# Attention in a hybrid decoder step: a fifth bank for scores, a per-partition scalar for GpSimd's scaling, and two small steps moved to GpSimd

## The chip, the core and the metric

The kernel runs on one core of a Trainium2 chip. The metric is the device time of one execution in microseconds (us), the median of several executions; lower is better.

## What is computed

One inference step of a two-layer decoder trunk, for a prompt of 2048 positions and eight samples of one position each. Layer 0 has a pooling mixer beside differential attention, layer 1 a gated delta rule beside a spatial-gating MLP. The change is in the attention of the prompt. For each of 6 heads there are two softmaxes, over two halves of the head's 128 channels, and their difference weighs the values:

```python
def diff_core(q, k, v, allowed, lam):
    s = jnp.einsum('bqhcd,bkhcd->bhcqk', q, k).astype(jnp.float32) * (DIFF_DH ** -0.5)
    p = jax.nn.softmax(jnp.where(allowed, s, -jnp.inf), axis=-1)
    attn = p[:, :, 0] - lam * p[:, :, 1]
    return jnp.einsum('bhqk,bkhd->bqhd', attn.astype(v.dtype), v)
```

Here c (0 or 1) is the softmax, and a query position sees the keys up to its own.

## The kernel before

The stages run one after the other: the input projection of layer 0, the attention of the prompt, the output projection of layer 0, then layer 1. The code is written in program order, and a scheduler sets the final order on each engine; every engine works its own queue strictly in that order. TensorE is called PE, VectorE DVE, ScalarE ACT, GpSimd POOL.

`attention` loops over 6 heads and, in each, over 16 query tiles of 128 positions. A tile i needs i+1 blocks of 128 keys, which `attn_tile` takes in 1 to 4 chunks (nch) of up to 512 keys. So of a head's 16 tiles four have one chunk, four have two, four three and four four: 240 chunks in all, and 72 tiles with more than one chunk.

For each chunk and each of the two softmaxes: PE multiplies queries by keys into a bank of PSUM (`sc`, lines 810 and 811, and a mask for the last chunk, 813). DVE takes the negated row maximum of it (`nb`, line 814). ACT writes the exponentials to `p` in SBUF and their sums to `l` (line 815). The chunks of a tile are then weighed against each other by the factors `cf`, an array of 128 partitions by 2 softmaxes by nch chunks, which the code calls f. With more than one chunk DVE takes the minimum m of nb (826), subtracts (827), ACT takes the exponential (828), DVE multiplies the sums by it (830), adds them (831), inverts (832), multiplies the second softmax's inverse by minus lambda (833) and multiplies the factors by the inverses (834).

Then, for each chunk, POOL multiplies the second softmax's half of `p` by its factor (838). For three chunks in four DVE multiplies the first half by its factor and adds the second half in one instruction (841); for the fourth POOL does both (843 and 844). PE transposes the result into a bank `tr` (848), ACT copies it to SBUF (850), and PE multiplies it by the values into a bank `pv` (852), which DVE copies out (853). After every fourth tile `attn_out` transposes four finished tiles into a bank `ot` (785), and ACT scales them (787).

PSUM has eight banks. In the table AT a letter is a bank, but X and Y are two banks each; a kind takes the letters of its string in turn, so scores go through X, X, D and A, where the two X are the two banks in turn.

Of the kernel before, what the change touches and what calls it, by code (L numbers as in the profile page):

```python
# [10 lines left out]
F32 = mybir.dt.float32  # L11
# [4 lines left out]
ALU = mybir.AluOpType  # L16
# [4 lines left out]
P = 128  # L21
# [24 lines left out]
BO, BR, BU = 2, 2, 4  # L46
DORD = (("out", 6), ("step", 5), ("merge16", 3), ("merge", 3), ("front", 1), ("blocks", 1), ("load", 0))
SP = 0
AT = dict(sc="XXDA", tr="Y", pv="B", ot="C")
W1, W2, WA, WB, WC = "P", "D", "P", "PD", "PD"  # L50
DE = "PDPPPPP"
CM = 1
# [11 lines left out]
class Net:  # L64
# [634 lines left out]
    def lam_const(self):  # L699
        nc, I, c = self.nc, self.I, self.const  # L700
        tmp = ExitStack()
        t = self.pool(tmp, "lam", 1)
        lq = t.tile([P, 4, 64], F32, name="lq")
        nc.sync.dma_start(lq, I["lam_qk"].rearrange("a c d -> a (c d)").broadcast_to([P, 256]))
        pr = t.tile([P, 2, 64], F32, name="lpr")
        for i in range(2):
            nc.vector.tensor_tensor(pr[:, i], lq[:, 2 * i], lq[:, 2 * i + 1], ALU.mult)
        e = c.tile([P, 2], F32, name="lexp")
        nc.vector.tensor_reduce(e, pr, AX.X, ALU.add)
        nc.scalar.activation(e, e, AF.Exp)  # L710

        self.nlam = c.tile([P, 1], F32, name="nlam")
        nc.vector.scalar_tensor_tensor(self.nlam, e[:, 1:2], -LAM0, e[:, 0:1], ALU.add, ALU.subtract)
        tmp.close()
        self.sub_w = c.tile([P, 1], F32, name="subw")
        nc.sync.dma_start(self.sub_w, I["subln_w"].rearrange("a d -> d a"), allow_slow_non_contiguous=True)

        nc.vector.tensor_scalar(self.sub_w, self.sub_w, 0.5 * (1.0 - LAM0), None, ALU.mult)
        self.at = c.tile([P, NS, self.NJ, NH], F32, name="at")
        self.an8 = c.tile([NS, NH], F32, name="an8")  # L720
        self.tab = c.tile([1, NS * self.NJ], I32, name="tab")
        nc.sync.dma_start(self.tab, I["page_table"].rearrange("b j -> (b j)")[None, :])
        self.maskb = c.tile([P, P], BF16, name="maskb")
        nc.gpsimd.memset(self.maskb, 0.0)
        nc.gpsimd.affine_select(self.maskb, self.maskb, pattern=[[-1, P]], compare_op=ALU.is_ge, fill=NEG, base=0,
                                channel_multiplier=1)

    def attention(self):
        st = ExitStack()
        nc, I = self.nc, self.I  # L730
        self.banks = AT

# [58 lines left out]
    def attn_tile(self, i, kvt, qt, o, oss, pp, tp, sm):  # L791
        nc = self.nc
        mm = nc.tensor.matmul
        nk = i + 1
        nch = (nk + 3) // 4
        q0 = (i % 4) * P
        nb = sm.tile([P, 2, 4], F32, tag="nb", name="nb")
        l = sm.tile([P, 2, 4], F32, tag="l", name="l")
        pc = []
        with self.tc.high_priority(SP) if SP else nullcontext():  # L800
            for j in range(nch):
                n = min(512, nk * P - 512 * j)
                w = max(n, 256)
                kh, kl = kvt[j][:2]
                p = pp.tile([P, 2, 512], F32, tag="p", name="p")
                for c in range(2):
                    sc = self.bank("sc", 512)
                    qc = qt[:, c, q0:q0 + P]
                    last = j == nch - 1
                    mm(sc[:, :w], qc, kh[:, c, :w], start=True, stop=False)  # L810
                    mm(sc[:, :w], qc, kl[:, c, :w], start=False, stop=not last)  # L811
                    if last:
                        mm(sc[:, n - P:n], self.identb, self.maskb, start=False, stop=True)
                    nc.vector.tensor_reduce(nb[:, c, j:j + 1], sc[:, :n], AX.X, ALU.max, negate=True)  # L814
                    nc.scalar.activation(p[:, c, :n], sc[:, :n], AF.Exp, bias=nb[:, c, j:j + 1],  # L815
                                         accum_out=l[:, c, j:j + 1])
                pc.append((p, n))
        cf = sm.tile([P, 2, 4], F32, tag="cf", name="cf")
        f = cf[:, :, :nch]
        if nch == 1:  # L820
            nc.vector.reciprocal(f, l[:, :, :1])
            nc.vector.tensor_scalar(f[:, 1, :], f[:, 1, :], self.nlam, None, ALU.mult)
        else:
            r = sm.tile([P, 2], F32, tag="r", name="r")
            m = sm.tile([P, 2], F32, tag="m", name="m")
            nc.vector.tensor_reduce(m, nb[:, :, :nch], AX.X, ALU.min)
            nc.vector.tensor_tensor(f, m[:, :, None].broadcast_to([P, 2, nch]), nb[:, :, :nch], ALU.subtract)
            nc.scalar.activation(f, f, AF.Exp)
            lf = l[:, :, :nch]
            nc.vector.tensor_tensor(lf, lf, f, ALU.mult)  # L830
            nc.vector.tensor_reduce(r, lf, AX.X, ALU.add)
            nc.vector.reciprocal(r, r)
            nc.vector.tensor_scalar(r[:, 1:2], r[:, 1:2], self.nlam, None, ALU.mult)
            nc.vector.tensor_tensor(f, f, r[:, :, None].broadcast_to([P, 2, nch]), ALU.mult)  # L834
        pv = self.bank("pv", P)
        for j in range(nch):
            p, n = pc[j]
            nc.gpsimd.tensor_tensor(p[:, 1, :n], p[:, 1, :n], cf[:, 1, j:j + 1].broadcast_to([P, n]), ALU.mult)  # L838
            turn = self.turn()
            if turn % 4 < 3:  # L840
                nc.vector.scalar_tensor_tensor(p[:, 0, :n], p[:, 0, :n], cf[:, 0, j:j + 1], p[:, 1, :n], ALU.mult, ALU.add)  # L841
            else:
                nc.gpsimd.tensor_tensor(p[:, 0, :n], p[:, 0, :n], cf[:, 0, j:j + 1].broadcast_to([P, n]), ALU.mult)
                nc.gpsimd.tensor_tensor(p[:, 0, :n], p[:, 0, :n], p[:, 1, :n], ALU.add)
            pt = self.bank("tr", 4, P)
            nt = n // P
            for t in range(nt):
                nc.tensor.transpose(pt[:, t, :], p[:, 0, t * P:t * P + P], self.ident)
            tt = tp.tile([P, 4, P], F32, tag="pt", name="pt")
            nc.scalar.copy(tt[:, :nt, :], pt[:, :nt, :])  # L850
            for t in range(nt):
                mm(pv, tt[:, t, :], kvt[j][2][:, t, :], start=j == 0 and t == 0, stop=j * 4 + t == nk - 1)  # L852
        nc.vector.tensor_copy(o, pv)
        junk = sm.tile([P, P], F32, tag="junk", name="junk", bufs=2)
        nc.scalar.activation(junk, pv, AF.Square, scale=P ** -0.5, accum_out=oss)  # L855
# [917 lines left out]
```

## Time and profile before

| What | Value |
|---|---|
| median of 3 runs | 3105.16 us (3101.53 to 3109.34) |
| the profiled execution's own time | 3097.32 us |
| its span, first to last instruction | 3095.6 us |
| PE busy over the span | 2800.3 us (90%) |
| DVE busy | 2073.9 us (67%) |
| ACT busy | 1492.5 us (48%) |
| POOL busy | 1663.1 us (54%) |

The span is that of the one execution that the profiler recorded; the time of an execution is 1.7 us longer than its span here. The busy shares are means over stages of different kinds: the attention lies from about 781 to 1390 us of the span. Outside it the change adds two small instructions that make a constant; the scheduler's order also differs in parts of layer 1, whose code is the same. A line of a group or a timeline reads: line, engine, operation, output<-inputs, shape out<-in, count, then times.

### The profile page before, as it was taken

How to read it: one execution, taken by the hardware profiler on the slowest of the kernel's cores; microseconds unless marked ns; L12 is line 12 of the kernel's file. 1: busy time of each engine (PE TensorE's matmuls, PEld its weight loads, DVE VectorE, ACT ScalarE, POOL GpSimd, SP SyncE). 2: the span in 40 equal slices, each digit the busy share in tenths (PEclk: the TensorE clock that was granted, in tenths of full speed). 3: DMA queues.
4: the chain of work that ended last, by engine and by line, in shares of the span. 5: the costliest groups of instructions: out<-in, count | busy, mean ns of one | idle time of the engine just before them, and what ended most of it. 6: DMA issues, size and time to landing. Idle time of an engine off the chain costs nothing. (4 is left out here: it accounts for less than half of the span.)

```text
span 3095.6 us, 57877 instructions
## 1 busy us (share of the span) xinstructions
PE 2800.3 (90%) x20425; PEld 2541.6 (82%) x20425; DVE 2073.9 (67%) x4067; ACT 1492.5 (48%) x4431; POOL 1663.1 (54%) x1223
## 2 busy tenths in 40 slices
PE   8999899999998898989898888999999899858999
PEld 8999798999777777778787878778889888747887
DVE  5465555564898999885677877567787574347662
ACT  6644245534887787762223224455454443334431
POOL 4576546571567866664576654546443244246541
PEclk9999999999999999999999999999999999969999
DMA  4567766655344424217777655435233244468442
GB/s 163 166 197 252 246 217 204 189 183 172 86 106 113 103 62 106 71 54 228 228 248 213 183 179 168 132 105 149 88 88 99 90 94 126 114 168 237 134 126 91
DMA packets 428061, 462.55 MB, mean 149 GB/s; under 512 B 84987, under 2 KB 338340, under 8 KB 427772
## 3 DMA queue, kind: packets, MB, share of 16 engines
q1 hardware_dynamic: 427772, 458.86, 50.0%
q8 instruction: 162, 2.65, 0.4%
q14 instruction: 127, 1.04, 0.1%
HBM read 332.41 MB, written 126.33 MB: 148 GB/s over the span
## 5 line engine op out<-in xcount | busy, mean ns | idle before, releaser
L186 PE MATMUL acc<-bh,whi 128*128 128x346 f32 (+6 forms) x2072 | 689.7, 333 | 42.0 <-DVE cx L1232 32.2
L188 PE MATMUL acc<-bh,wlo 128*128 128x346 f32 (+6 forms) x2072 | 687.3, 332 | 8.8 <-DVE wlo L167 8.2
L187 PE MATMUL acc<-bl,whi 128*128 128x346 f32 (+6 forms) x2072 | 686.3, 331 | 0.0
L186 PEld LDWEIGHTS acc<-bh,whi 128*128 128x128 f32 x2072 | 396.9, 192 | 64.8 <-issue 40.8
L188 PEld LDWEIGHTS acc<-bh,wlo 128*128 128x128 f32 x2072 | 396.4, 191 | 28.3 <-DVE wlo L167 10.2
L187 PEld LDWEIGHTS acc<-bl,whi 128*128 128x128 f32 x2072 | 397.0, 192 | 16.6 <-issue 3.1
L815 ACT ACTIVATE p<-sc,nb 128x512 f32<-128x512 f32 (+3 forms) x480 | 302.0, 642 | 72.8 <-DVE nb L814 62.0
L838 POOL TENSOR_TENSOR p<-p,cf 128x512 f32<-128x512 f32 (+3 forms) x240 | 236.9, 1005 | 184.0 <-DVE cf L834 49.5
L167 POOL TENSOR_TENSOR wlo<-wraw,whi 128x1024 fp32r<-128x1024 f32 (+1 forms) x90 | 218.6, 2432 | 138.7 <-ACT whi L165 138.4
L814 DVE TENSOR_REDUCE nb<-sc 128x1 f32<-128x512 f32 (+3 forms) x480 | 275.8, 597 | 18.5 <-PE sc L811 8.9
L628 POOL TENSOR_TENSOR kp<-kp,at 128x768 f32<-128x768 f32 x120 | 203.0, 1701 | 156.4 <-DMA kp<-in_cache_v 130.2
L550 POOL TENSOR_TENSOR kp<-kp,qb 128x768 f32<-128x768 f32 x88 | 169.7, 1934 | 178.3 <-DMA kp<-in_cache_k 140.2
L186 PE MATMUL acc<-whi,bh 128*128 128x256 f32 x864 | 249.9, 290 | 0.3 <-DVE th L418 0.3
L187 PE MATMUL acc<-wlo,bh 128*128 128x256 f32 x864 | 248.6, 288 | 0.2 <-POOL wlo L167 0.2
L188 PE MATMUL acc<-whi,bl 128*128 128x256 f32 x864 | 248.7, 288 | 0.0
L630 DVE TENSOR_TENSOR sacc<-sacc,kp 128x768 f32<-128x768 f32 x120 | 180.2, 1502 | 83.7 <-POOL kp L628 71.5
L852 PE MATMUL pv<-v,pt 128*128 128x128 f32 x1632 | 220.2, 283 | 15.1 <-ACT pt L850 8.2
L810 PE MATMUL sc<-kh,q 128*128 128x512 f32 (+2 forms) x480 | 211.1, 440 | 23.8 <-ACT p L815 20.6
L852 PEld LDWEIGHTS pv<-v,pt 128*128 128x128 f32 x1632 | 203.8, 196 | 29.9 <-ACT junk L855 13.9
L165 ACT CAST whi<-wraw 128x1024 fp32r<-128x1024 f32 (+1 forms) x124 | 129.9, 1048 | 142.9 <-DMA wraw<-in_w_in_e 50.3
L841 DVE SCALAR_TENSOR_TENSOR p<-p,cf 128x512 f32<-128x512 f32 (+3 forms) x180 | 190.6, 1062 | 7.3 <-POOL p L838 6.6
L551 DVE TENSOR_REDUCE sc<-kp 128x12 f32<-128x768 f32 x128 | 119.1, 946 | 96.4 <-POOL kp L550 95.8
(439 smaller groups left out, 7506.8 us busy)
## 6 DMA issues: line engine op xcount, KB each, us to landing
kp<-in_cache_k SPq DMA_DIRECT2D x128, 384.0 KB
kp<-in_cache_v SPq DMA_DIRECT2D x128, 384.0 KB
wraw<-in_w_in_e SPq DMA_DIRECT2D x56, 512.0 KB
wraw<-in_w_in_o SPq DMA_DIRECT2D x56, 512.0 KB
mc<-cat SPq DMA_DIRECT2D x72, 256.0 KB
mg<-sg SPq DMA_DIRECT2D x72, 256.0 KB
kh<-kh SPq DMA_DIRECT2D x48, 256.0 KB
kl<-kl SPq DMA_DIRECT2D x48, 256.0 KB
```

What stands on the lines that cost most here:

```text
L167: e.tensor_tensor(lo, raw, hi.bitcast(F32), ALU.subtract)
L186: mm(out, ah, bh, start=first, stop=False)
L187: mm(out, ah, bl, start=False, stop=False)
L188: mm(out, al, bh, start=False, stop=last)
L628: nc.gpsimd.tensor_tensor(h3(w), h3(v), self.at[:, b, j, :, None].broadcast_to([P, NH, P]), ALU.mult)
L630: nc.vector.tensor_tensor(acc, acc, v, ALU.add)
L810: mm(sc[:, :w], qc, kh[:, c, :w], start=True, stop=False)
L814: nc.vector.tensor_reduce(nb[:, c, j:j + 1], sc[:, :n], AX.X, ALU.max, negate=True)
L815: nc.scalar.activation(p[:, c, :n], sc[:, :n], AF.Exp, bias=nb[:, c, j:j + 1], accum_out=l[:, c, j:j + 1])
L838: nc.gpsimd.tensor_tensor(p[:, 1, :n], p[:, 1, :n], cf[:, 1, j:j + 1].broadcast_to([P, n]), ALU.mult)
L841: nc.vector.scalar_tensor_tensor(p[:, 0, :n], p[:, 0, :n], cf[:, 0, j:j + 1], p[:, 1, :n], ALU.mult, ALU.add)
L852: mm(pv, tt[:, t, :], kvt[j][2][:, t, :], start=j == 0 and t == 0, stop=j * 4 + t == nk - 1)
```

## The change

Four things change. The scores get a fifth bank, C, which was that of `ot`; `ot` now shares the two Y banks with `tr`. POOL's scaling of `p` (lines 838 and 843 of before) is written as a tensor_scalar, with the factor as a scalar for each partition, where it was a tensor_tensor with the factor broadcast along the row. The subtraction that makes the factors (827) moves from DVE to POOL. The multiplication by minus lambda (833, of one column, on DVE) becomes a multiplication of all factors by a constant `nl2` of two columns, 1 and minus lambda, on POOL; it stands after the product of line 830, which reads the factors as they were.

```diff
-AT = dict(sc="XXDA", tr="Y", pv="B", ot="C")
+AT = dict(sc="XXDAC", tr="Y", pv="B", ot="Y")
...
+        self.nl2 = c.tile([P, 2], F32, name="nl2")
+        nc.gpsimd.memset(self.nl2, 1.0)
+        nc.vector.tensor_copy(self.nl2[:, 1:2], self.nlam)
...
-            nc.vector.tensor_tensor(f, m[:, :, None].broadcast_to([P, 2, nch]), nb[:, :, :nch], ALU.subtract)
+            nc.gpsimd.tensor_tensor(f, m[:, :, None].broadcast_to([P, 2, nch]), nb[:, :, :nch], ALU.subtract)
             nc.scalar.activation(f, f, AF.Exp)
             lf = l[:, :, :nch]
             nc.vector.tensor_tensor(lf, lf, f, ALU.mult)
+            nc.gpsimd.tensor_tensor(f, f, self.nl2[:, :, None].broadcast_to([P, 2, nch]), ALU.mult)
             nc.vector.tensor_reduce(r, lf, AX.X, ALU.add)
             nc.vector.reciprocal(r, r)
-            nc.vector.tensor_scalar(r[:, 1:2], r[:, 1:2], self.nlam, None, ALU.mult)
             nc.vector.tensor_tensor(f, f, r[:, :, None].broadcast_to([P, 2, nch]), ALU.mult)
...
-            nc.gpsimd.tensor_tensor(p[:, 1, :n], p[:, 1, :n], cf[:, 1, j:j + 1].broadcast_to([P, n]), ALU.mult)
-            turn = self.turn()
-            if turn % 4 < 3:
+            nc.gpsimd.tensor_scalar(p[:, 1, :n], p[:, 1, :n], cf[:, 1, j:j + 1], None, ALU.mult)
+            if self.turn() % 4 < 3:
                 nc.vector.scalar_tensor_tensor(p[:, 0, :n], p[:, 0, :n], cf[:, 0, j:j + 1], p[:, 1, :n], ALU.mult, ALU.add)
             else:
-                nc.gpsimd.tensor_tensor(p[:, 0, :n], p[:, 0, :n], cf[:, 0, j:j + 1].broadcast_to([P, n]), ALU.mult)
+                nc.gpsimd.tensor_scalar(p[:, 0, :n], p[:, 0, :n], cf[:, 0, j:j + 1], None, ALU.mult)
                 nc.gpsimd.tensor_tensor(p[:, 0, :n], p[:, 0, :n], p[:, 1, :n], ALU.add)
```

The lines of after are 3 or 4 higher: the scaling stands at 842 and 846, the add at 847, the moved subtraction at 831, the new product at 835, the DVE steps at 830 (m), 834 (sums by factors), 836, 837 and 838 (factors by inverses), the score maximum at 818, and DVE's scaling and add at 844.

The scheduler moves instructions with it. These are POOL's rows of before at tile 12 of the third head; each p is a chunk's buffer, and cf_12435 is that tile's array of factors.

```order
L838 TENSOR_TENSOR p_12314<-p_12314,cf_12327 128x512
L844 TENSOR_TENSOR p_12303<-p_12303 128x512
L838 TENSOR_TENSOR p_12389<-p_12389,cf_12435 128x512
L838 TENSOR_TENSOR p_12400<-p_12400,cf_12435 128x512
L838 TENSOR_TENSOR p_12411<-p_12411,cf_12435 128x512
L843 TENSOR_TENSOR p_12411<-p_12411,cf_12435 128x512
L838 TENSOR_TENSOR p_12422<-p_12422,cf_12435 128x128
L844 TENSOR_TENSOR p_12411<-p_12411 128x512
```

And these are POOL's rows at the same tile after the change, where its factors are cf_12438, and those of the two tiles behind it cf_12556 and cf_12668.

```order
L831 TENSOR_TENSOR cf_12438<-m_12440,nb_12390 128x8
L835 TENSOR_TENSOR cf_12438<-cf_12438,nl2_354 128x8
L842 TENSOR_SCALAR p_12392<-p_12392,cf_12438 128x512
L842 TENSOR_SCALAR p_12403<-p_12403,cf_12438 128x512
L842 TENSOR_SCALAR p_12414<-p_12414,cf_12438 128x512
L846 TENSOR_SCALAR p_12414<-p_12414,cf_12438 128x512
L842 TENSOR_SCALAR p_12425<-p_12425,cf_12438 128x128
L831 TENSOR_TENSOR cf_12556<-m_12558,nb_12508 128x8
L847 TENSOR_TENSOR p_12414<-p_12414 128x512
L779 TENSOR_TENSOR ob_12021<-ob_12021,ss_12020 128x512
L831 TENSOR_TENSOR cf_12668<-m_12670,nb_12620 128x8
L835 TENSOR_TENSOR cf_12556<-cf_12556,nl2_354 128x8
```

The five scalings of the tile stand in the same order; ahead of them POOL now has the tile's two small steps (831 and 835), at this tile with nothing between them. The next tile's two steps stand behind all five scalings, with the add, line 779's product of `ob` and the step 831 of the tile after it between them.

DVE's rows of before at the same tile, from its minimum m to the finished factors, are these; the rows of nb_12505, p and ob belong to other tiles.

```order
L826 TENSOR_REDUCE m_12437<-nb_12387 128x2
L827 TENSOR_TENSOR cf_12435<-m_12437,nb_12387 128x8
L841 SCALAR_TENSOR_TENSOR p_12292<-p_12292,cf_12327 128x512
L853 COPY ob_12018<-pv_12161 128x128
L830 TENSOR_TENSOR l_12388<-l_12388,cf_12435 128x8
L814 TENSOR_REDUCE nb_12505<-sc_12513 128x1
L831 TENSOR_REDUCE r_12436<-l_12388 128x2
L814 TENSOR_REDUCE nb_12505<-sc_12519 128x1
L832 RECIPROCAL r_12436<-r_12436 128x2
```

And DVE's rows from the same minimum after the change:

```order
L830 TENSOR_REDUCE m_12440<-nb_12390 128x2
L856 COPY ob_12021<-pv_12164 128x128
L818 TENSOR_REDUCE nb_12508<-sc_12511 128x1
L844 SCALAR_TENSOR_TENSOR p_12317<-p_12317,cf_12330 128x512
L818 TENSOR_REDUCE nb_12508<-sc_12516 128x1
L818 TENSOR_REDUCE nb_12508<-sc_12522 128x1
L818 TENSOR_REDUCE nb_12508<-sc_12527 128x1
L818 TENSOR_REDUCE nb_12508<-sc_12533 128x1
L834 TENSOR_TENSOR l_12391<-l_12391,cf_12438 128x8
L836 TENSOR_REDUCE r_12439<-l_12391 128x2
L837 RECIPROCAL r_12439<-r_12439 128x2
L838 TENSOR_TENSOR cf_12438<-cf_12438,r_12439 128x8
```

Between the minimum and the product that reads the exponentials DVE now has five score maxima of the next tile, where it had none, and the four steps that finish the factors follow each other.

## Rows read from the trace of the kernel before

**Rows 1.** Busy time of each engine in the attention (us, instruction counts, clock, DMA).

```profile
781.00:1390.00 609.00, 548.30 (x3700) 453.97 (x3698) 555.50 (x1310) 473.46 (x1550) 421.91 (x396) 0.98 0.32 85
```

**Rows 2.** Groups by form, DVE, 781 to 1390 us: busy us, mean ns, idle before.

```profile
L814 DVE TENSOR_REDUCE nb<-sc 128x1 f32<-128x512 f32 x336 | 222.0, 677 | 11.9 <-PE sc L811 8.9 <-PE sc L813 1.9
L841 DVE SCALAR_TENSOR_TENSOR p<-p,cf 128x512 f32<-128x512 f32 x119 | 136.9, 1154 | 5.0 <-POOL p L838 4.6
L833 DVE TENSOR_SCALAR r<-r,nlam 128x1 f32<-128x1 f32 x72 | 14.8, 205 | 0.7
L827 DVE TENSOR_TENSOR cf<-m,nb 128x8 f32<-128x8 f32 x24 | 10.9, 454 | 0.3
L827 DVE TENSOR_TENSOR cf<-m,nb 128x6 f32<-128x6 f32 x24 | 9.2, 385 | 0.1
L827 DVE TENSOR_TENSOR cf<-m,nb 128x4 f32<-128x4 f32 x24 | 8.9, 371 | 0.2
L830 DVE TENSOR_TENSOR l<-l,cf 128x6 f32<-128x6 f32 x24 | 12.3, 511 | 0.3 <-ACT cf L828 0.3
```

**Rows 3.** Timeline of POOL in the attention: start us, duration us.

```profile
1143.76 1.04 POOL L843 TENSOR_TENSOR p<-p,cf 128x512 f32<-128x512 f32 x1
1144.76 1.49 POOL L838 TENSOR_TENSOR p<-p,cf 128x512 f32<-128x512 f32 x1
1153.76 0.39 POOL L838 TENSOR_TENSOR p<-p,cf 128x128 f32<-128x128 f32 x1
1154.12 1.27 POOL L844 TENSOR_TENSOR p<-p 128x512 f32<-128x512 f32 x1
```

**Rows 4.** Timeline of DVE at the same place.

```profile
1143.13 0.70 DVE L827 TENSOR_TENSOR cf<-m,nb 128x8 f32<-128x8 f32 x1
1143.75 1.60 DVE L841 SCALAR_TENSOR_TENSOR p<-p,cf 128x512 f32<-128x512 f32 x1
1145.48 0.80 DVE L830 TENSOR_TENSOR l<-l,cf 128x8 f32<-128x8 f32 x1
1147.29 0.75 DVE L841 SCALAR_TENSOR_TENSOR p<-p,cf 128x512 f32<-128x512 f32 x1
1148.57 0.15 DVE L834 TENSOR_TENSOR cf<-cf,r 128x8 f32<-128x8 f32 x1
```

**Rows 5.** Groups by form, POOL, 781 to 1390 us.

```profile
L838 POOL TENSOR_TENSOR p<-p,cf 128x512 f32<-128x512 f32 x168 | 188.6, 1139 | 138.0 <-DVE cf L834 49.5 <-PE tr L848 18.4 <-PE sc L811 13.0
L844 POOL TENSOR_TENSOR p<-p 128x512 f32<-128x512 f32 x49 | 67.0, 1368 | 0.1
L843 POOL TENSOR_TENSOR p<-p,cf 128x512 f32<-128x512 f32 x49 | 60.6, 1236 | 0.0
```

**Rows 6.** Waits in the attention: total us, times, longest us.

```profile
POOL p L838 <- DVE cf L834: 49.5, 28, 5.6
PE sc L810 <- ACT p L815: 20.6, 39, 4.1
DVE nb L814 <- PE sc L811: 8.9, 10, 3.0
DVE nb L814 <- PE sc L813: 8.3, 11, 1.8
```

**Rows 7.** Groups by form, POOL, whole span: operations with few inputs or columns.

```profile
L125 POOL TENSOR_SCALAR vss<-vss 128x16 f32<-128x16 f32 x4 | 1.1, 272 | 27.5 <-DVE vss L1037 27.5
L125 POOL TENSOR_SCALAR arena<-arena 128x96 f32<-128x96 f32 x1 | 0.5, 455 | 0.0
L246 POOL TENSOR_SCALAR qkw<-qkw 128x128 f32<-128x128 f32 x1 | 0.5, 549 | 0.0
L972 POOL TENSOR_SCALAR_AFFINE_SELECT wst<-wst 128x512 f32<-128x512 f32 x1 | 0.6, 639 | 0.0
L892 POOL TENSOR_TENSOR mc<-mc,mg 128x32 f32<-128x32 f32 x2 | 0.5, 254 | 0.2 <-DMA mg<-sg 0.2
```

**Rows 8.** Instructions on tile p: ns min/median/max, first and last start us, sampled forms.

```profile
L838 POOL TENSOR_TENSOR p<-p,cf x240: 392/1039/1490, 785.4 to 1379.4; 128x512 f32<-128x512 f32 x98, 128x128 f32<-128x128 f32 x10, 128x384 f32<-128x384 f32 x10, 128x256 f32<-128x256 f32 x2
```

## Prediction

> **What bounds the kernel now.** I read the attention by itself, since the change lies there. First the busy time of each engine in that stretch [rows 1]: of 609 us DVE works 555.5 (91%), PE 548.3, ACT 473.5 and POOL 421.9 (69%), at a granted clock of 0.98. DVE is the fullest engine; PE is close behind. POOL has 187 us to spare.
>
> Then what DVE's 555 us are made of [rows 2]. The score maxima of 512 columns are 222 us, which the change leaves as they are. But one and the same instruction takes very different times elsewhere: the scaling and add of 512 columns takes 1154 ns on average and 0.75 us in one of the timeline's rows, and the tiny differences and products of 4 to 8 columns take 371 to 511 ns on average, while one of them takes 0.15 us in another [rows 2, 4].
>
> The two timelines side by side show why [rows 3, 4]. DVE's scaling and add starts at 1143.75 and ends at 1145.35; POOL runs a scaling from 1143.76 to 1144.80. DVE moves only when POOL's instruction is over, and is done 0.55 us later. POOL's next one, started at 1144.76, lasts 1.49 us where the one before took 1.04: it waits the 0.45 us in which DVE works. So a DVE instruction with two inputs in SBUF and a POOL instruction exclude each other for their whole length. DVE's busy time holds waits for POOL, and a longer POOL instruction is a longer wait for DVE. Time on POOL is therefore not free, although POOL is the least busy of the four engines.
>
> Last the waits [rows 6]. POOL waits 49.5 us for finished factors, in 28 stretches. PE waits 20.6 us until ACT has read a score bank, and DVE waits 8.9 + 8.3 = 17.2 us for PE's scores.
>
> **The change, part by part. The scalar per partition** is the part that decides, and the trace doesn't show it: no tensor_scalar with an array as scalar, and none of 512 columns, runs on POOL before. It shows the same operation with a constant [rows 7]: 272 ns at 16 columns (four executions) and 455 ns at 96, which is (455 - 272) / 80 = 2.29 ns a column. The broadcast form takes 0.39 us at 128 and 1.04 us at 512 columns [rows 3], or 1.69 ns a column. Continued, the tensor_scalar takes 0.53, 0.82, 1.11 and 1.41 us at 128, 256, 384 and 512 columns, against 0.39, 0.61, 0.82 and 1.04. The bounds: the row of 128 columns, 549 ns, gives 2.47 ns a column and 1.50 us at 512; another operation with one input, line 972's select, takes 639 ns at 512. Between these I take 1.41, since it comes from the operation itself and two of its sizes, and the third size lies above the line, not below.
>
> The numbers of the scalings are those of lines 838 and 843: 168 + 49 = 217 of 512 columns [rows 5], and 29, 25 and 29 of 384, 256 and 128 (counted from the loop: 24 each on line 838, and 5, 1 and 5 on line 843). So the change adds 217 x 0.37 + 29 x 0.29 + 25 x 0.21 + 29 x 0.14 = 98 us to POOL.
>
> The Trainium skill, GPSIMD Engine Reference, section 4.1 (Engine selection), says the opposite: on GpSimd an operation with one input runs at about line rate, and one with two inputs is the slow one. Worked out from its 1.2 GHz, 512 columns are an estimated 0.43 us and a start; with some 0.2 us for that, the sum by the rule would be about the first rival's, 3056 us, where the rows' sum is 3145. Line 972's row agrees with the rule, the three tensor_scalar rows don't.
>
> **The two moved steps** are 72 subtractions and 72 products of 4 to 8 columns on POOL. The nearest rows are 254 ns at 32 columns with two inputs [rows 7] and, continuing the broadcast form down to 8 columns, 0.39 - 120 x 0.00169 = 0.19 us. I take 0.2, together 29 us on POOL. DVE loses 10.9 + 9.2 + 8.9 = 29.0 us of subtractions and 14.8 us of line 833 [rows 2], 44 us in all. None of this adds or moves a DMA; SP's queue isn't touched.
>
> **The new waits.** A tile's subtraction now stands in POOL's queue behind the scalings of the tile before, and the new product behind the subtraction, an ACT exponential and a DVE product. ACT's next score exponentials stand behind that exponential, DVE's next maxima behind that product. In the timeline the subtraction ends at 1143.83 and the DVE product that reads the exponential at 1145.48 + 0.80 = 1146.28, 2.45 us later [rows 4]. At most tiles the order puts an add (1.27 us [rows 3]) or more between POOL's two steps, at some nothing. So POOL stands still for 0 to 2.4 us a tile; I take 0.7, half of what an add leaves open, or 72 x 0.7 = 50 us.
>
> **More meetings with DVE.** The excess over the undisturbed length is now about 0.10 x 168 + 0.20 x 49 + 0.10 x 49 = 32 us (1139, 1236 and 1368 ns against 1.04, 1.04 and 1.27 us [rows 3, 5]). If POOL hardly rests, each of DVE's 180 scalings and adds costs it the 0.45 us, the 61 narrower ones about 0.25: 54 + 15 = 69 us, 37 more.
>
> **The banks.** The fifth score bank lets PE run one chunk's half further ahead. That can give back at most the 17.2 us for which DVE waits for scores [rows 6], and nothing where POOL sets the pace; I take nothing. `ot` in the Y banks keeps one of two transpose banks busy for four transposes and ACT's copy of them, 24 times: at worst it eats PE's 60.7 us of idle time [rows 1], at best nothing, and while POOL sets the pace PE's idle time covers it; nothing again. The constant costs two small instructions early in the kernel, under DVE's work there. Layer 1's altered order has no price in any row; I allow 8 us to either side.
>
> **The sum.** POOL's time in the attention: 422 + 98 + 29 + 37 = 586 us, 50 of waits, and 13 us at the two ends, where POOL has nothing yet or nothing any more (its first scaling starts at 785.4, its last at 1379.4 [rows 8], of 781 to 1390). That makes 649 us, against 609 now: 40 us more. The check on DVE: 555 - 44, and for its 180 meetings waits of 0.4 us that grow with POOL's length (1.36) and its share of time (69% to about 90%), 0.31 us more each or 55 us, and 20 for the tiny products: 586, under 649. So POOL takes over the end from DVE. The profiled 3097.3 becomes 3137; by the median of the runs, which lies 8 us above that execution, 3145 us.
>
> **The rivals.** *The scalar form at one-input rate* (faster): POOL's scalings take the 0.64 us of line 972 [rows 7] instead of 1.04, about 100 us less, 29 more for the two steps: 351. DVE's waits for POOL shrink with it, 555 - 44 - 46 = 465. Then ACT's 473 and PE's 548 are left [rows 1], and the attention ends at about 560: 3056 us. For it: line 972. Against it: each of the three tensor_scalar rows. It decides below a price of about 1.0 us at 512 columns; the stage gets longer above about 1.26, where the 98 us are 58 and POOL's sum is 609. *The scalar form as the broadcast form*, 1.04 us: POOL 422 + 29 + 50 of waits = 501, DVE 511 and its waits as before; the 44 us come out by a third, 3090 us, or are lost in POOL's new waits, 3105. *The new waits bind all three engines*: if the 2.4 us are open at each tile, 72 x 1.7 more is 122 us, of which the DVE work that is placed there hides about half: 3205 us. For it: DVE's last step waits for POOL's product with only two small steps ahead of it. *The fifth bank is the gain*: PE is held for banks, 20.6 us [rows 6]; with DVE relieved the 17 us come out and nothing else: 3088 us; this needs a cheap scaling, and I count it with the second rival.
>
> **How the numbers follow.** The forecast's own case has 0.58, its range by the bounds is 3115 to 3190 (price 1.41 to 1.50, waits 0.3 to 1.2 us a tile). The one-input rate has 0.2, the broadcast price 0.12 (half faster, half within 0.3%), the binding waits 0.1. That makes faster 0.26, the same 0.06, slower 0.68; 0.3%, or 9 us, is about what a measurement of this kernel tells from no change. The range has to reach into the first rival and stops short of the last one: 3060 to 3195 us.
>
> **What would show it.** Right: POOL's tensor_scalar of 512 columns at 1.3 us or more, POOL over 85% busy in an attention of about 650 us, DVE's scaling and add above 1.15 us on average, ACT and DVE waiting for lines 831 and 835. Wrong: a tensor_scalar under 1.0 us, and DVE's scaling and add under a microsecond; or a high price with an unchanged stage, which would mean that POOL's spare time hid it after all.

## The result, and the profile after

The changed kernel took 3201.7 us (median of 4 runs, 3197.4 to 3206.0), the kernel before 3103.4 us on the same chip (3095.9 to 3109.3): a ratio of 1.032, interval 1.030 to 1.034. The direction was forecast, the size was not: +40 us were predicted and +98 came, and the time lies 7 us above the range of 3060 to 3195 us.

Nearly the whole loss is in the attention: its first to its last matmul took 613 us before and take 710 us now, 97 of the 100 us by which the profiled span grew (3195.7 us now). The busy time of each engine over the stage, in the columns of [rows 1]:

```profile
780.00:1491.00 711.00, 581.16 (x3700) 487.56 (x3699) 507.47 (x1165) 478.62 (x1552) 565.21 (x541) 0.91 0.27 72
```

POOL, the fifth of the five busy times, went from 422 to 565 us, but that is 79% of the stage: it stands still for 146 us. DVE fell from 555.5 to 507.5. No engine is full, and the granted clock of TensorE fell from 0.98 to 0.91.

POOL's groups by form in the stage, as in [rows 5]:

```profile
L842 POOL TENSOR_SCALAR p<-p,cf 128x512 f32<-128x512 f32 x168 | 262.7, 1573 | 61.3 <-DVE cf L838 33.3 <-PE tr L851 10.4 <-PE sc L815 3.4
L846 POOL TENSOR_SCALAR p<-p,cf 128x512 f32<-128x512 f32 x49 | 79.0, 1612 | 0.0
...
L842 POOL TENSOR_SCALAR p<-p,cf 128x384 f32<-128x384 f32 x24 | 29.8, 1243 | 0.0
...
L842 POOL TENSOR_SCALAR p<-p,cf 128x256 f32<-128x256 f32 x24 | 22.3, 929 | 4.5 <-ACT p L819 2.3 <-DVE cf L826 2.2
L842 POOL TENSOR_SCALAR p<-p,cf 128x128 f32<-128x128 f32 x24 | 14.5, 603 | 37.3 <-ACT p L819 36.2 <-DVE cf L826 1.1
...
L835 POOL TENSOR_TENSOR cf<-cf,nl 128x8 f32<-128x8 f32 x24 | 4.8, 200 | 12.4 <-DVE l L834 12.2
```

The scalar form takes 1.57 us at 512 columns, where the broadcast form took 1.04 undisturbed. DVE's groups by form, as in [rows 2]:

```profile
L818 DVE TENSOR_REDUCE nb<-sc 128x1 f32<-128x512 f32 x336 | 221.7, 681 | 52.3 <-PE sc L815 34.3 <-PE sc L817 16.6
L844 DVE SCALAR_TENSOR_TENSOR p<-p,cf 128x512 f32<-128x512 f32 x119 | 119.6, 1005 | 51.6 <-POOL p L842 51.5
```

The scaling and add became shorter, 1005 ns where it was 1154, although each POOL scaling is longer. And DVE now stands idle 52 us ahead of its score maxima, nearly all of it for scores, which are PE's work; before, that was 11.9 [rows 2]. So PE is late. PE's groups in the stage show where it stands still (behind the second bar: idle time ahead of the group, and what ended it):

```profile
L855 PE MATMUL pv<-v,pt 128*128 128x128 f32 x1630 | 236.0, 293 | 22.0 <-ACT pt L853 15.5 <-ACT junk L858 5.5
L814 PE MATMUL sc<-kh,q 128*128 128x512 f32 (+2 forms) x464 | 206.2, 445 | 10.6 <-ACT p L819 9.6 <-ACT pt L853 0.3
L815 PE MATMUL sc<-kl,q 128*128 128x512 f32 (+2 forms) x464 | 174.3, 378 | 4.1 <-DMA kl<-kl 4.1
L851 PE MATMUL tr<-ident,p 128*128 128x128 f32 x815 | 145.1, 304 | 45.2 <-POOL p L847 26.6 <-DVE cf L838 5.0 <-ACT o L791 4.2
...
L789 PE MATMUL ot<-ident,ob 128*128 128x128 f32 x96 | 19.9, 343 | 46.3 <-POOL ob L779 46.3
```

In the kernel before, the same groups were idle for 15.1, 22.4, 2.8, 18.3 and 0.7 us. Its rows of tr and ot:

```profile
L848 PE MATMUL tr<-ident,p 128*128 128x128 f32 x815 | 128.2, 278 | 18.3 <-DVE p L841 11.0 <-POOL p L844 4.4 <-DVE r L832 1.7
L785 PE MATMUL ot<-ident,ob 128*128 128x128 f32 x96 | 14.7, 274 | 0.7 <-POOL ob L775 0.7
```

Two lines make the difference, and POOL releases both: the transposes of ot wait for POOL's scaling of ob (L779), those of tr for POOL's add (L847).

A stretch in which PE stands still because the next instruction of its queue waits is called a hold below. One of them, seen from POOL (timeline: start us, duration us):

```profile
1063.44 5.72 POOL L842 TENSOR_SCALAR p<-p,cf 128x512 f32<-128x512 f32 x4 [0.20 <-DVE cf L838]
1069.15 1.55 POOL L846 TENSOR_SCALAR p<-p,cf 128x512 f32<-128x512 f32 x1
1070.69 2.78 POOL L842 TENSOR_SCALAR p<-p,cf 128x512 f32<-128x512 f32 x2
1073.44 0.19 POOL L831 TENSOR_TENSOR cf<-m,nb 128x6 f32<-128x6 f32 x1
1073.60 1.29 POOL L878 TENSOR_TENSOR wo512l<-wr,wo512h 128x512 fp32r<-128x512 f32 x1
1074.82 1.07 POOL L779 TENSOR_TENSOR ob<-ob,ss 128x512 f32<-128x512 f32 x1
1075.81 1.30 POOL L847 TENSOR_TENSOR p<-p 128x512 f32<-128x512 f32 x1
```

The same place on PE:

```profile
1068.76 0.40 PE L815 MATMUL sc<-kl,q 128*128 128x512 f32 x1
1075.94 1.11 PE L789 MATMUL ot<-ident,ob 128*128 128x128 f32 x4 [6.78 <-POOL ob L779]
```

And the busy times and clock around it (columns of [rows 1]):

```profile
1060.00:1069.00 9.00, 8.90 (x58) 6.83 (x56) 8.41 (x23) 7.73 (x26) 7.19 (x7) 1.00 0.30 90
1069.00:1076.00 7.00, 0.22 (x2) 0.06 (x2) 4.59 (x5) 0.57 (x3) 7.00 (x8) 0.79 0.00 1
1076.00:1083.00 7.00, 6.07 (x26) 5.47 (x26) 3.29 (x7) 5.00 (x13) 6.04 (x6) 0.50 0.36 112
1083.00:1089.00 6.00, 6.00 (x44) 5.32 (x43) 4.14 (x10) 5.68 (x19) 5.39 (x5) 0.98 0.11 33
```

POOL has no gap, works through its queue in order, and comes to ob at 1074.82. PE, whose queue is in order too, does nothing else meanwhile: 6.78 us. Then it pays again: after the hold the granted clock is 0.50, the lower of the two levels (1.2 GHz), for 7 us, and near 1.00 (2.4 GHz) only from 1083 on.

### The profile page after: what moved, and what is told of

The parts are those of the page before. It is cut to its first block, busy times and chain, and to the rows that moved or that the text cites. A ratio compares the mean times of both kernels' runs of the same rounds, so it can differ in the third digit from the quotient of the medians.

```text
span 3195.7 us, 57790 instructions
## 1 busy us (share of the span) xinstructions
PE 2831.8 (89%) x20425; PEld 2579.0 (81%) x20425; DVE 2024.7 (63%) x3924; ACT 1496.8 (47%) x4431; POOL 1807.2 (57%) x1368
## 3 DMA queue, kind: packets, MB, share of 16 engines
q14 instruction: 127, 1.04, 0.1%
## 5 line engine op out<-in xcount | busy, mean ns | idle before, releaser
L842 POOL TENSOR_SCALAR p<-p,cf 128x512 f32<-128x512 f32 (+3 forms) x240 | 328.5, 1379 | 103.1 <-ACT p L819 38.4
L855 PE MATMUL pv<-v,pt 128*128 128x128 f32 x1632 | 236.4, 293 | 22.0 <-ACT pt L853 15.5
L855 PEld LDWEIGHTS pv<-v,pt 128*128 128x128 f32 x1632 | 219.0, 205 | 40.9 <-ACT pt L853 26.9
L844 DVE SCALAR_TENSOR_TENSOR p<-p,cf 128x512 f32<-128x512 f32 (+3 forms) x180 | 162.2, 905 | 55.7 <-POOL p L842 55.3
L851 PE MATMUL tr<-ident,p 128*128 128x128 f32 x816 | 145.3, 304 | 45.2 <-POOL p L847 26.6
```

Of the source, the lines that this page charges most:

```text
L842: nc.gpsimd.tensor_scalar(p[:, 1, :n], p[:, 1, :n], cf[:, 1, j:j + 1], None, ALU.mult)
```

## The experiments

Three theories, one for each part. **A:** the price of the scalar form makes the loss. **B:** the new waits of the two steps make it. **C:** the banks make it, because PE is held at the transposes of ot. Ratios are to the kernel before on the same chip, with their 95% intervals. Where PE's idle time is given, it is summed from the matmul records between the first and the last one of the attention.

**One part at a time: e1_scalar, e2_steps, e3_banks, e4_steps_banks.** Each is the kernel before with a piece of the diff above:

```diff
 e1_scalar (lines 838 and 843):
-            nc.gpsimd.tensor_tensor(p[:, 1, :n], p[:, 1, :n], cf[:, 1, j:j + 1].broadcast_to([P, n]), ALU.mult)
+            nc.gpsimd.tensor_scalar(p[:, 1, :n], p[:, 1, :n], cf[:, 1, j:j + 1], None, ALU.mult)
 e2_steps: nl2, and
-            nc.vector.tensor_tensor(f, m[:, :, None].broadcast_to([P, 2, nch]), nb[:, :, :nch], ALU.subtract)
+            nc.gpsimd.tensor_tensor(f, m[:, :, None].broadcast_to([P, 2, nch]), nb[:, :, :nch], ALU.subtract)
+            nc.gpsimd.tensor_tensor(f, f, self.nl2[:, :, None].broadcast_to([P, 2, nch]), ALU.mult)
-            nc.vector.tensor_scalar(r[:, 1:2], r[:, 1:2], self.nlam, None, ALU.mult)
 e3_banks:
-AT = dict(sc="XXDA", tr="Y", pv="B", ot="C")
+AT = dict(sc="XXDAC", tr="Y", pv="B", ot="Y")
 e4_steps_banks: the last two together
```

> Of the change only the scaling by a scalar per partition; the steps and the banks are as before. Theory A (the price of the scalar form makes nearly all of the +98 us): 300 scalings cost POOL about 0.53 us more each at 512 columns, some 140 us in all, and the time is 3180 to 3205 us. Theory B (the new waits of the two steps make it): POOL had 187 us to spare, so the dearer scaling is hidden or half hidden, 3100 to 3125 us. Theory C (PE held at the transposes of ot, because they share banks with tr): no change from the banks here, 3100 to 3140 us. In all of them the scaling of 512 columns is near 1.57 us, and DVE's scaling and add of 512 columns under 1.1 us on average, since DVE is held for less of a tensor_scalar than of a tensor_tensor.

Measured: 3149.9 us, 1.017 (1.013 to 1.020), the attention 669 us. By the ratio that is some 52 us, by the medians 58: above B's and C's ranges, below A's, and about half of what A expected. POOL's extra 0.53 us per scaling costs, but not one for one. PE's group of tr waits 42.6 us for POOL's add, where it waited 4.4 before:

```profile
L848 PE MATMUL tr<-ident,p 128*128 128x128 f32 x816 | 133.3, 291 | 46.1 <-POOL p L844 42.6 <-DVE p L841 2.0 <-ACT pt L850 0.8
```

> Of the change only the two steps of the chunk factors on POOL; scaling by the broadcast form, banks as before. Theory A (price of the scalar form): 29 us more on POOL, 44 us less on DVE, 3090 to 3115 us. Theory B (new waits of the two steps): ACT waits some 50 us for POOL's subtraction and DVE some 30 us for POOL's product, as after the whole change, and the time is 3160 to 3200 us. Theory C (banks): 3090 to 3115 us, like A.

Measured: 3091.1 us, 0.999 (0.998 to 1.001). B is wrong for the steps by themselves: ACT waits only 7.1 us for POOL's subtraction. Nor does DVE's relief show in the time: between 780 and 1390 us it is busy for 533 us, where it was 556.

> Of the change only the banks: five for the scores, ot in the banks of tr. Theory C (PE held at the transposes of ot for POOL's work on ob): PE waits 30 us or more at line 789, and the time is 3130 to 3160 us. Theories A and B: the hold needs a POOL that runs late, and POOL is early here, so 3085 to 3108 us, the lower end if the fifth bank takes away DVE's 17 us of waits for scores.

Measured: 3148.4 us, 1.017 (1.015 to 1.020), as much as the scalar form. POOL has no more work here than before, and still PE's group of ot reads:

```profile
L785 PE MATMUL ot<-ident,ob 128*128 128x128 f32 x96 | 19.3, 336 | 29.7 <-POOL ob L775 29.7
```

> The whole change but for the scalar form: scalings by the broadcast form at 1.04 us. Theory A (price): the loss is gone, 3085 to 3115 us. Theory B (waits of the two steps): 3165 to 3200 us. Theory C (banks): 3130 to 3165 us, with PE's wait at line 789 still at 30 us or more. If two parts only cost together, this one stays near 3103 and the one with the scalar form alone also falls short of 3200.

Measured: 3145.9 us, 1.017 (1.014 to 1.020), with 40.1 us idle ahead of ot: C's case, and nothing from the steps.

**What of the banks: f1_share, f2_banks_later.**

```diff
 f1_share:
-AT = dict(sc="XXDA", tr="Y", pv="B", ot="C")
+AT = dict(sc="XXDA", tr="Y", pv="B", ot="Y")
 f2_banks_later: the banks as in the change, and
-                if done:
+                if done and n % 4 == 1:
                     self.attn_out(*done, sm)
```

> The kernel before, with ot in the banks of tr and bank C left unused: the scores keep four banks. Theory C1 (the loss of the banks part is the shared rotation, which fixes ot's place between the transposes of the tiles): PE waits about 30 us at line 785 for POOL's ob, as with five banks, and the time is 3135 to 3160 us. Theory C2 (the fifth score bank itself costs: PE runs ahead with scores and leaves the transposes late): 3085 to 3105 us.

Measured: 3148.3 us, 1.013 (1.010 to 1.016), 15.9 us idle ahead of ot. By the whole time, sharing alone costs most of the part. The attention itself is only 25 us longer than before, where e3_banks has 45; what else the whole time lost lies outside it, and no run shows why. So the fifth score bank is not free either, as C2 has it in part, and it took no wait away: PE waits 20.5 us in e3_banks until ACT has read a score bank, and waited 20.6 before [rows 6].

> The banks part as in the change, but ot's transposes and store are issued one tile later, when POOL's scaling of ob is long over. Theory C1: PE's wait at line 785 falls under 5 us and the time is back at 3080 to 3105 us, at the lower end if the fifth score bank then gives its 17 us. Theory C2: the loss stays, 3130 to 3160 us.

Measured: 3130.1 us, 1.008 (1.006 to 1.011). Half of the loss is gone: neither C1's whole return nor C2's whole loss. PE's groups:

```profile
L848 PE MATMUL tr<-ident,p 128*128 128x128 f32 x816 | 135.2, 287 | 23.3 <-POOL p L844 11.3 <-ACT o L787 7.8 <-DVE p L841 2.8
L785 PE MATMUL ot<-ident,ob 128*128 128x128 f32 x96 | 16.8, 302 | 10.3 <-POOL ob L775 10.3
```

The order of PE's records tells more. Counted for the first eight times, so many transposes of tr stand between the last one of the four tiles and those of ot:

```
before (ot in C)        5  19  13  14  26  27  21  19
e3_banks, f1_share      5   9  13   1   5   9  13   1
f2_banks_later         11  19  27   3  11  19  27   3
```

With a bank of its own, in the kernel before, ot stands where POOL's ob is ready: the scheduler could put it further back. In the rotation of tr it stands just behind the next tile's transposes, where it is issued; where that tile is a head's first, that is a single one. There PE waits for POOL, but not by the count alone. Of the 29.7 us of e3_banks, 7.6 are at the four places with 1, 5.1 at the five with 5, 12.5 at the five with 9, nothing at those with 13, and 4.5 in the last head; of the 15.9 us of f1_share, 8.4 are at those with 1. Issued a tile later, ot hardly waits at the places with 3 (0.4 us); of the 10.3 us that stay, 6.5 are at two of those with 11 and 3.4 in the last head.

**Which chunks the scalar form costs in: g1_scalar_dve, g2_scalar_pool.**

```diff
+            turn = self.turn()
+            if turn % 4 < 3:     # g1_scalar_dve; g2_scalar_pool: turn % 4 == 3, and line 843 too
+                nc.gpsimd.tensor_scalar(p[:, 1, :n], p[:, 1, :n], cf[:, 1, j:j + 1], None, ALU.mult)
+            else:
+                nc.gpsimd.tensor_tensor(p[:, 1, :n], p[:, 1, :n], cf[:, 1, j:j + 1].broadcast_to([P, n]), ALU.mult)
```

> The kernel before, with the scalar form only in the 180 chunks whose add is DVE's: 180 of the 300 scalings, about 85 of the 145 us that the scalar form adds to POOL. Theory A1 (the loss follows POOL's total time): 60% of the loss of the scalar form alone, 3120 to 3130 us. Theory A2 (the loss comes from the 60 chunks that POOL finishes alone, scaling, scaling, add, where PE waited 43 us for the add): no loss, 3085 to 3105 us.

Measured: 3099.9 us, 0.998 (0.996 to 1.000), although POOL's busy time between 780 and 1390 us rose from 421.9 to 495.3 us. A1 is wrong. PE's transposes wait 9.2 us for POOL's add, not 42.6.

> The kernel before, with the scalar form only in the 60 chunks that POOL finishes alone: 120 of the 300 scalings, about 60 of the 145 us on POOL. Theory A1 (POOL's total time): 40% of the loss, 3110 to 3120 us. Theory A2 (the chain of three POOL instructions in such a chunk, 4.5 us where it took 3.3): nearly the whole loss, 3135 to 3155 us, with PE waiting some 40 us at line 848 for line 844's add.

Measured: 3139.2 us, 1.011 (1.008 to 1.013), the attention 658 us of e1_scalar's 669. A2 was nearer, but the 16.7 us in which tr waits for the add fall short of its 40; ot waits 15.6 us for ob here, with a bank of its own. The hold isn't always at the same line.

**Both holds, and the price: h1_scalar_noadd, h2_g1_steps, h3_after_ob_dve, h4_const.** The last one leaves out the first factor in the 60 chunks that POOL finishes alone, and has a constant in its place, to price the two.

```diff
 h1_scalar_noadd: the scalar form, and
-            if turn % 4 < 3:
+            if turn % 4 < 4:
 h2_g1_steps: g1_scalar_dve with the two steps
 h3_after_ob_dve: the whole change, and
-                    nc.gpsimd.tensor_tensor(ob, ob, ss[:, :, None].broadcast_to([P, 4, P]), ALU.mult)
+                    nc.vector.tensor_tensor(ob, ob, ss[:, :, None].broadcast_to([P, 4, P]), ALU.mult)
 h4_const: the scalar form, and at line 843
+                nc.gpsimd.tensor_scalar(p[:, 0, :n], p[:, 0, :n], 0.5, None, ALU.mult)
```

> The kernel before with the scalar form in all chunks, and with POOL's adds given to DVE: 240 scalings and no add on POOL, 240 scalings and adds on DVE. Theory A2 (the chunks that POOL finishes alone make the loss): PE's wait of 43 us at the transposes for POOL's add is gone, the attention is about as long as before, 3075 to 3115 us, with POOL busy about 420 us and DVE about 530 us in it. Theory A1' (any chunk that waits for a 1.57 us scaling pays): a loss stays, 3125 to 3150 us.

Measured: 3080.1 us, 0.991 (0.988 to 0.993): faster than both kernels, with the dear form in every chunk. The attention takes 582 us. Its PE group of tr, and its DVE group of 512 columns:

```profile
L848 PE MATMUL tr<-ident,p 128*128 128x128 f32 x815 | 130.3, 277 | 6.8 <-DVE p L841 4.5 <-DVE r L831 1.1 <-DVE cf L834 0.6
```

```profile
L841 DVE SCALAR_TENSOR_TENSOR p<-p,cf 128x512 f32<-128x512 f32 x168 | 134.4, 800 | 0.0
```

> The kernel before with the two steps on POOL and the scalar form only in the chunks whose add is DVE's; banks as before. Each of these alone cost nothing, and DVE gains from both. If they add up, 3080 to 3100 us. If POOL's extra time and its extra steps only cost together, 3115 us or more.

Measured: 3149.3 us, 1.014 (1.011 to 1.016). The second case: two edits that cost nothing apart cost 1.4% together. PE waits 22.2 us at tr for POOL's add and 28.4 us at pv for ACT's copies of pt.

> The whole change, with the scaling of ob on DVE and no longer on POOL (24 instructions of 512 columns). If PE is held at ot because POOL comes late to ob, the 46 us of PE's idle time ahead of ot shrink to 15 us or less and the time falls by 30 to 50 us, to 3150 to 3170 us. If ot's place in the order alone costs, whoever scales ob, PE's idle time ahead of ot stays above 30 us and the time above 3185 us.

Measured: 3184.4 us, 1.025 (1.022 to 1.027), against 1.032 of the whole change. The idle time ahead of ot fell from 46.3 to 9.9 us, so POOL's lateness was its cause, as in the first case. But that ahead of pv rose from 22.0 to 41.3 us, and PE's idle time in all fell only from 129 to 118: most of the hold moved on, and the time misses the first case's range.

> The kernel before with the scalar form in all chunks, where the scaling by the first factor in the chunks that POOL finishes alone uses the constant 0.5 in place of the factor (so these chunks are not scaled by their own factor). It sets the price of a scalar per partition beside that of a constant in one execution. If reading a scalar per partition is what is dear: 1.41 us at 512 columns by the constant (the forecast's line through the three constant rows) and 1.57 by the scalar. If the operation itself is dear: 1.55 to 1.62 us by both. The time is near that of the scalar form alone, 3140 to 3170 us.

Measured: 3137.0 us, 1.010 (1.007 to 1.013). POOL's groups of 384 and 128 columns, with a scalar per partition (L838) and with a constant (L843):

```profile
L838 POOL TENSOR_SCALAR p<-p,cf 128x384 f32<-128x384 f32 x24 | 30.8, 1283 | 0.8 <-PE sc L813 0.8
...
L838 POOL TENSOR_SCALAR p<-p,cf 128x128 f32<-128x128 f32 x24 | 14.9, 622 | 39.4 <-ACT p L815 35.4 <-DVE r L832 4.1
L843 POOL TENSOR_SCALAR p<-p 128x384 f32<-128x384 f32 x5 | 5.9, 1170 | 0.5 <-ACT p L815 0.5
...
L843 POOL TENSOR_SCALAR p<-p 128x128 f32<-128x128 f32 x5 | 2.6, 529 | 0.0
```

The operation itself is dear: (1170 - 529) / 256 = 2.50 ns a column, an estimated 1.49 us at 512, and the rows of 512 columns have means of 1594 ns with the constant and 1620 ns with the scalar. At 128 and 384 columns the scalar per partition adds 0.09 and 0.11 us.

**The remaining combinations and two controls: e5_scalar_banks, e6_scalar_steps, c1_noadd, k1_after_noadd.** The first two leave one part out of the change; the others are h1's edit (`turn % 4 < 4`) made in the kernel before and in the changed one.

> The whole change without the two steps. If the parts add up (scalar form +1.7%, banks +1.7%, steps nothing), about +3.3%, 3195 to 3215 us, and the steps cost nothing here either. If the steps are what holds the others' work back (as with the scalar form in DVE's chunks alone, where they cost 1.3%), this one falls short of the whole change by 20 us or more, 3150 to 3180 us.

Measured: 3205.0 us, 1.036 (1.032 to 1.040): the first case, the parts add up.

> The whole change without the banks. If the parts add up, as the scalar form alone, 3145 to 3165 us. If scalar form and steps cost together, 3175 to 3205 us, and of the banks' loss little is left in the whole change.

Measured: 3173.4 us, 1.027 (1.023 to 1.031), nearly the second case. With the scalar form, the steps do cost, about 1%, and on top of both the banks add only some 0.5% in the whole change (1.030 to 1.034, whose interval meets this one's). PE's group of tr:

```profile
L851 PE MATMUL tr<-ident,p 128*128 128x128 f32 x816 | 136.4, 293 | 60.2 <-POOL p L847 42.1 <-DVE p L844 7.2 <-DVE l L833 4.1
```

> The kernel before with POOL's adds given to DVE and the scalings by the broadcast form: the control to the same with the scalar form, which was 0.93% faster than before. If that gain came from the three-instruction chunks alone, 3070 to 3090 us here too. If it needs the scalar form, which holds DVE for 0.45 us at most, then DVE's 240 scalings and adds at 1.15 us bring it over the length of the stage, and it takes 3110 to 3140 us.

Measured: 3088.6 us, 0.999 (0.997 to 1.001). The time alone is inside the first case's range, but the kernel before took 3091.7 us on this chip: there is no gain. PE's idle time ahead of tr rises from 18.3 to 27.9 us, mostly for DVE, and that ahead of pv falls from 15.1 to 6.4. In the same groups as for h1_scalar_noadd, PE first and DVE behind it:

```profile
L848 PE MATMUL tr<-ident,p 128*128 128x128 f32 x815 | 132.5, 282 | 27.9 <-DVE p L841 20.7 <-DVE r L831 2.2 <-DVE m L826 2.0
```

```profile
L841 DVE SCALAR_TENSOR_TENSOR p<-p,cf 128x512 f32<-128x512 f32 x168 | 175.8, 1050 | 14.4 <-POOL p L838 14.0
```

So h1's gain needs the scalar form: it lets DVE finish its scaling and add in 800 ns where the broadcast form makes it 1050, and PE's transposes wait for DVE the shorter.

> The whole change with POOL's adds given to DVE. If POOL's three-instruction chunks are what makes POOL late for everything that PE waits for, ob and the subtraction among it, nearly the whole loss is gone: 3070 to 3110 us. If the shared banks cost by ot's place in the order alone, their part stays: 3125 to 3150 us.

Measured: 3132.0 us, 1.013 (1.009 to 1.016): the banks' part stays, with 33.4 us idle ahead of ot, although POOL is busy for 391 us of 610.

**The rest of the holds: l1_h1_steps, l2_k1_later.** h1 with the two steps, and k1 with ot a tile later.

> The two steps on POOL added to the fastest version so far (scalar form, POOL's adds on DVE, banks as before, 0.93% faster than before). If the steps only cost by the POOL work queued around them, and POOL is free for a third of the stage here, DVE's relief comes out or is neutral: 3060 to 3090 us. If the round trip over three engines is what costs, whatever POOL has to do, 3095 us or more.

Measured: 3083.7 us, 0.996 (0.994 to 0.998): still faster than before, but h1 without the steps was at 0.991. PE's group of pv tells what is late (7.3 us idle in h1):

```profile
L856 PE MATMUL pv<-v,pt 128*128 128x128 f32 x1632 | 227.6, 283 | 30.7 <-ACT pt L854 27.4 <-ACT junk L859 3.2
```

> The whole change with POOL's adds on DVE and ot's transposes issued one tile later: both holds of PE that the runs found are taken away, and the fifth score bank is kept. If the fifth bank is worth the 17 to 31 us for which PE or DVE wait for score banks, 3060 to 3085 us. If sharing the banks goes on costing elsewhere (tr's turn behind ACT's read of ot), 3095 to 3130 us.

Measured: 3115.7 us, 1.006 (1.004 to 1.008), 10.2 us idle ahead of ot and 25.9 ahead of pv. The time is the second case's, but its reason, tr behind ACT's read of ot, accounts for only 2.7 us of PE's idle time. No run showed a gain from the fifth score bank, here or in e3_banks against f1_share.

**All runs together.** PE's idle time in the attention beside the attention's length, from each kernel's profiled execution (us):

```
kernel            PE idle  length   ratio of the whole time
h1_scalar_noadd      46      582    0.991
e2_steps             60      608    0.999
before               61      613    1
l1_h1_steps          62      606    0.996
c1_noadd             63      615    0.999
g1_scalar_dve        64      615    0.998
l2_k1_later          73      626    1.006
f2_banks_later       75      628    1.008
h4_const             75      633    1.010
f1_share             75      639    1.013
h2_g1_steps          83      647    1.014
e3_banks             91      658    1.017
k1_after_noadd       92      652    1.013
e4_steps_banks       93      654    1.017
g2_scalar_pool       94      658    1.011
e1_scalar            96      669    1.017
e6_scalar_steps     117      690    1.027
h3_after_ob_dve     118      685    1.025
after               129      710    1.032
e5_scalar_banks     134      708    1.036
```

A straight line through the twenty is 524 us + 1.42 times the idle time. One of the 1.42 is the idle time itself. The other 0.42 is PE's own busy time, 552 us before and 581 after for the same matmuls. That goes with the slower clock behind a hold, as in the four windows above: between the two levels, a mean of 0.91 over 711 us is an estimated 128 us at the lower one, and 0.98 over 609 us [rows 1] some 24. The length is that of one execution, on several chips; the attention's part and the whole time's change agree to within 18 us.

## Why the prediction was wrong

**What bounds the stage** is the step that failed. The prediction took POOL to set the end once its time passed DVE's, and added terms of POOL time to a sum of 649 us. PE sets it: its busy time and the holds of its in-order queue. POOL's busy time came out near, 586 forecast and 565 measured, but the stage became 710, not 649. And that the 586 came near is luck: the price was 43 us too low, and some 70 us of meetings with DVE (32 already there, 37 more) are, by the sum, all but absent: 422 - 32 + 141 + 36 = 567. A rise of POOL's busy time cost nothing in g1_scalar_dve and 1.7% in e1_scalar; what differs is PE's wait for POOL's add, 9.2 against 42.6 us. And DVE, the fullest engine before, was relieved in e2_steps without a gain.

**The banks: "nothing again"** is the term that cost most beside its forecast: 1.7% alone, some 54 us, 45 of them in the attention, though only some 0.5% on top of the other two parts. The prediction named the shared Y banks and let PE's idle time of 60.7 us cover them. That idle time was no cover: a hold adds to it, and lowers the clock on top. What it overlooked is that the scheduler could put ot further back while it had bank C, which its 0.7 us of idle time in the trace of before reflects, and that in tr's rotation it stands where it is issued.

**The scalar form: 98 us of POOL time.** The sign was right, the price low: 0.53, 0.42, 0.32 and 0.21 us more at 512, 384, 256 and 128 columns instead of 0.37, 0.29, 0.21 and 0.14, together 217 x 0.53 + 29 x 0.42 + 25 x 0.32 + 29 x 0.21 = 141 us. The line through 16 and 96 columns was too flat (2.29 ns a column, measured 2.50), and the row of 128 columns had said so [rows 7]. But as time of the kernel the form cost 52 us alone (1.7% of 3092), most of it (45 of 56 us in the attention) found again where only the 60 chunks have it that POOL finishes by itself, scaling, scaling, add. The rule of the Trainium skill that was weighed there (GPSIMD Engine Reference, section 4.1, Engine selection), one-input operations at about line rate, is contradicted by this trace: 1573 ns at 512 columns.

**More meetings with DVE: 37 us, and DVE's waits growing with POOL's length.** Wrong in sign. A tensor_scalar on POOL does not keep DVE's scaling and add out as the tensor_tensor did, and DVE's busy time fell to 507 us, where the check had 586.

**The two steps: 29 us and 50 us of waits.** The price was a little low: 200 to 316 ns by the size, 36 us in all. The 50 us contain a slip: half of what an add leaves open is (2.45 - 1.27) / 2 = 0.59 us a tile, not 0.7, or 42 us. The waits cost nothing by themselves (e2_steps) and about 1% beside the scalar form (e6_scalar_steps): ACT waits 7.1 us for the subtraction in the first and 49.9 in the second. They come when POOL's queue ahead of the subtraction is long, and then ACT brings pt late to PE (39.5 us idle ahead of pv in e6_scalar_steps, 30.2 in e1_scalar). On top of scalar form and banks no further cost is to be seen (1.036 without them, 1.032 with).

**The rivals.** "The new waits bind all three engines" gave 3205 us, near the measured time, but for a reason that the runs don't support: that case was built on the steps, which alone cost nothing. Scalar form and banks alone add up to 3.4%, against 3.2% measured. "The fifth bank is the gain" found no support: it took none of PE's 20.6 us of waits away (e3_banks). The range was also narrower than its own bounds: price and waits both at their upper ends add up to 3145 + 23 + 36 = 3204 us, not 3190. That sum would have covered the measured time, for the wrong reason. The marks set for the prediction came out accordingly: tensor_scalar above 1.3 us (yes), POOL over 85% busy in an attention of about 650 us (no, 79% of 710), DVE's scaling and add above 1.15 us (no, 1.005), ACT waiting for line 831's subtraction (yes, 50.7 us), DVE for line 835's product (no, 2.0 us).

Left open: the order of the instructions changes with each edit, and no run held it fixed while a duration changed. That PE is held where ot stands in the order, while POOL is late with ob, is shown by f1, f2 and h3; why so much of e3_banks' wait lies at the places with 9 transposes is not. How much of the scalar form's and the steps' joint loss comes from duration and how much from another order is open too.

## What to carry to other kernels

Where queues are in order and no engine is full, don't add up busy time on the engine that the change loads: ask which of its results the bound engine waits for next, what stands ahead of that result in its queue, and whether the scheduler is still free to put the waiter behind other work. A buffer of its own can be worth more by the order that it leaves free than by the space. A dearer instruction can still be the better one if it lets a neighbour through: h1_scalar_noadd beat both kernels by 0.9% and more, though the dear form alone lost 1.7% and the adds on DVE alone gained nothing.

## What the hardware showed beyond that

**DVE gets through beside a tensor_scalar, and is kept out by a tensor_tensor.** DVE's timeline at the place of the hold above:

```profile
1066.10 0.74 DVE L844 SCALAR_TENSOR_TENSOR p<-p,cf 128x512 f32<-128x512 f32 x1
...
1073.50 4.03 DVE L844 SCALAR_TENSOR_TENSOR p<-p,cf 128x384 f32<-128x384 f32 x1 [0.15 <-POOL p L842]
```

At 1066.10 POOL was in the middle of four scalar-form scalings without a gap (1063.44 to 1069.16), and DVE took its undisturbed 0.74 us. At 1073.50 POOL's four tensor_tensors came one behind another, to 1077.11, and DVE's narrower instruction lasted to 1077.53, over all of them. Over the whole kernel after, the 86 scalings and adds of 512 columns that met only tensor_scalars took 1.17 us at most, 0.72 at least and 0.98 on average, so they are slowed too; 65 of them began and ended inside a single tensor_scalar. Before, the 98 that met a tensor_tensor took 1.24 us on average and up to 2.84. The Trainium skill (SBUF — State Buffer, section "SBUF: two separate sides") describes the port that both engines share as a lock held for the whole instruction, the other fully blocked. The tensor_tensor rows agree; those of the tensor_scalar don't, since DVE could begin and end inside one.

**A tensor_scalar of GpSimd costs 1.5 times the broadcast tensor_tensor**, 1573 ns against 1.04 us at 512 columns, and of that the scalar per partition is the small part (in h4_const 529 ns with a constant against 622 ns at 128 columns).

**A hold is paid twice.** After PE's 6.78 us without work it ran the next 7 us at half its clock: granted 0.79 in the hold, 0.50 behind it, 0.98 in the 6 us after that.
